# VectorE's order written out in the weight groups and in the layer norm, two more wide groups per FFN, and one sum done by a transfer

## The chip, the cores and the metric

The kernel runs on one NeuronCore of a Trainium2 chip. The metric is the device time of one execution in microseconds, as the median of three executions. The engines are PE (TensorE: matmuls and transposes), ACT (ScalarE), DVE (VectorE), POOL (GpSimd) and SP (SyncE, which only issues transfers here). Each engine has its own list of instructions and works it off in the order in which the list stands.

## The reference

One decoder layer on 256 tokens of width 2048, all in float32: a half-step SwiGLU FFN, a token mixer with two attention branches, a second half-step SwiGLU FFN, and a layer norm after each of the three.

```
def _swiglu(x, w_gate, w_up, w_down):
    return (jax.nn.silu(x @ w_gate) * (x @ w_up)) @ w_down      # 2048 -> 2 x 5632 -> 2048
def _layer_norm(x, g, b):   # (x - mean) * rsqrt(var + eps) * g + b
x = LN1(ALPHA * x + 0.5 * swiglu1(x));  x = LN2(ALPHA * x + mixer(x));  x = LN3(ALPHA * x + 0.5 * swiglu2(x))
```

The last line is a summary of the layer's body. The mixer multiplies by one wide input matrix, runs latent attention and differential attention, gates both and multiplies by an output matrix. Nearly all work is matrix products of the 256 tokens with weights that are read once.

## The kernel before

**Precision.** A float32 product is made of three products of reduced-precision fp32r operands. Each weight tile is split into `hi` (a CAST on ACT, line 150) and `lo` (source minus `hi`, a TENSOR_TENSOR on DVE, line 151). For each k tile of 128 rows PE then runs `triple`: hi by hi (L203), hi by lo (L204), lo by hi (L205), each 512 columns wide. L203 needs only the cast; L204 needs DVE's split too.

**Units and the ring.** Weights come in *units*: a raw tile of 128 x 1024 (two k tiles of 512 columns) or, for a "third slice", 128 x 512 (one k tile). The split results go to a ring of six (hi, lo) pairs, so that the cast of a unit waits until PE has finished the unit six before it. `unit`, `advance` and `look` make the program run the loads three units and the splits four units ahead of the products. The framework's scheduler then sorts each engine's instructions by its own estimates of readiness, within what data and buffers force; the order on an engine is what it leaves, not the order of the source.

**Groups.** Gate and up weights lie in 22 blocks of 512 columns (256 of each). The first two blocks go through plain `project` calls, the other twenty through ten calls of `Hybrid.group`, p = 1 to 10, in each of the two FFNs. A group takes two blocks and both halves of the tokens. Over some k tiles it uses Strassen's seven products instead of eight ("sevens"); the rest are plain units. The order of the units is written as a string: `"15pp6p72q4q3q"` for a *wide* group, `"15pp6p7p2q4q3qq"` for one that is not. A digit is a product, `p` and `q` are plain units of the first and second block. Each product has slices: two of 1024 (k tiles 0 to 7) and, in a wide group, a third of 512 (k tiles 8 and 9, tiles `eraw`). So 6a, 6b, 6c below are the slices of product 6, and p1, p2, p3 are the plain units in order. A wide group has 177 matmuls, one that is not wide 180.

**Sums of weights.** Products 5, 6 and 4 need sums of weight blocks. They are made in place, one DVE addition for each slice (L392). Product 7's sum is made by an accumulating transfer that POOL issues (L394). In the mixer's `small` groups all sums are on DVE.

**Leaving a group.** When a bank of PSUM is finished, DVE adds a saved copy (`gus`, L801), ACT applies silu (`sg`, L785), DVE multiplies (`hb`, L789), and two steps of `later` afterwards `put_h` turns the result with a DVE transpose (L668) and stores it to DRAM by four transfers on POOL's queue (L670). ACT also makes a *seed* (L367): it starts one of the group's banks with minus another bank. `snap` (L354, L355) are copies of banks.

**Layer norm.** `LayerNorm.apply` (DVE: L746 and following, a few 128 x 1 operations with one square root on ACT, then four 128 x 512 operations at L764) normalizes one half of the tokens; the transposes at L633 on PE feed the next stage from it. `finish` (L769, L770) applies gain and bias to the residual's copy; it is called 12 to 15 steps later, and nothing on PE waits for it soon.

## Time and profile before

| quantity | value |
|---|---|
| median of three executions | 1984.71 us (1983.56 to 1985.17) |
| the profiled execution | 1982.88 us, span 1981.1 us |
| PE busy | 1961.8 us, 99% of the span |
| weight loads (PEld) busy | 1623.6 us, 82% |
| DVE busy | 1761.0 us, 89% |
| ACT busy | 1269.4 us, 64% |
| POOL busy | 294.6 us, 15% |
| mean granted clock of PE | 0.997 of full |

PE is busy nearly everywhere, so the time is the number of its instructions times their spacing, plus the places where it waits. The second engine by occupancy is DVE; in the groups of the FFNs it has almost no idle time. A busy share over the whole span hides that: the groups have to be read by themselves.

### The profile page before, as it was taken

What the parts mean: (1) busy time and instruction counts of PE and PEld (TensorE: products, weight loads), DVE (VectorE), ACT (ScalarE), POOL (GpSimd) and SP (SyncE); (2) the same over time, 40 slices, a digit from 0 to 9 for tenths busy, and PEclk for the clock granted to TensorE, in tenths of its full rate; (3) what the DMA queues carried; (4) which work ended last, traced back from release to release, by engine and by line L of the source; (5) the groups of instructions that cost most, each with busy time, mean ns of one, the idle gap of its engine ahead of it and who ended that gap; (6) DMA issues with size and microseconds to landing.
All of it is one profiled execution on the core that took longest, in us unless ns stands there. A gap on an engine that the chain in (4) does not pass through costs nothing.

```text
span 1981.1 us, 25579 instructions
## 1 busy us (share of the span) xinstructions
PE 1961.8 (99%) x8796; PEld 1623.6 (82%) x8796; DVE 1761.0 (89%) x2135; ACT 1269.4 (64%) x1639; POOL 294.6 (15%) x515
## 2 busy tenths in 40 slices
PE   9999999999999999999999999999999999999997
PEld 8888888888888897888888888878888888888886
DVE  7999999999898889998977686699999999998886
ACT  6666666677655666666667864566666666766552
POOL 0211112112100011002223130012112211121000
PEclk9999999999999999999999999999999999999999
DMA  8978888869677666677667677578898878687663
GB/s 314 284 241 279 284 238 247 239 212 329 244 235 243 202 243 225 226 254 260 217 198 256 216 236 264 185 256 271 244 290 260 247 239 244 208 325 251 238 215 124
DMA packets 144594, 484.63 MB, mean 245 GB/s; under 512 B 20640, under 2 KB 20688, under 8 KB 144464
## 3 DMA queue, kind: packets, MB, share of 16 engines
q1 hardware_dynamic: 112752, 389.60, 57.1%
q0 software_dynamic: 31712, 93.41, 17.9%
q8 instruction: 69, 1.13, 0.2%
q14 instruction: 61, 0.50, 0.1%
HBM read 454.08 MB, written 28.84 MB: 244 GB/s over the span
## 4 chain that ended last, share of the span: by engine, by line
PE 89%; DVE 6%; issue 3%; DMA 1%; POOL 0%; ACT 0%; SPq 0%; DVEq 0%; POOLq 0%; ACTq 0%
PE mm L204 28%; PE mm L205 28%; PE mm L203 28%; DVE wring L151 3%; DVE sraw L392 1%; PE tr L203 1%; PE tr L204 1%; PE tr L205 1%; DMA raw<-in_gu_dram 1%; PE tr L633 0%; DMA sraw<-in_wgm_dram 0%; PE tr L1134 0%; PE tr L1207 0%; PE tr L1209 0%; DMA hT<-blocks 0%
## 5 line engine op out<-in xcount | busy, mean ns | idle before, releaser
L150 ACT CAST wring<-raw 128x1024 fp32r<-128x1024 f32 (+2 forms) x475 | 491.4, 1038 | 344.9 <-PE mm L205 244.6
L151 DVE TENSOR_TENSOR wring<-raw,wring 128x1024 fp32r<-128x1024 f32 (+2 forms) x475 | 568.7, 1203 | 112.5 <-ACT wring L150 104.9
L150 ACT CAST wring<-sraw 128x1024 fp32r<-128x1024 f32 x436 | 455.4, 1052 | 207.7 <-PE mm L205 73.2
L151 DVE TENSOR_TENSOR wring<-sraw,wring 128x1024 fp32r<-128x1024 f32 x436 | 525.9, 1222 | 25.5 <-ACT wring L150 21.4
L205 PE MATMUL mm<-wring,h 128*128 128x512 f32 (+2 forms) x1260 | 485.0, 385 | 0.0
L203 PE MATMUL mm<-wring,h 128*128 128x512 f32 (+2 forms) x1260 | 484.7, 385 | 0.0
L204 PE MATMUL mm<-wring,h 128*128 128x512 f32 (+2 forms) x1260 | 484.6, 385 | 0.0
L204 PE MATMUL mm<-wring,xs 128*128 128x512 f32 x776 | 303.1, 391 | 2.5 <-DVE wring L151 2.4
L203 PE MATMUL mm<-wring,xs 128*128 128x512 f32 x776 | 302.3, 390 | 0.0
L205 PE MATMUL mm<-wring,xs 128*128 128x512 f32 x776 | 302.1, 389 | 0.0
L205 PEld LDWEIGHTS mm<-wring,h 128*128 128x128 f32 x1260 | 236.7, 188 | 47.4 <-DVE h L151 0.9
L203 PEld LDWEIGHTS mm<-wring,h 128*128 128x128 f32 x1260 | 236.9, 188 | 46.9 <-ACT h L150 0.4
L204 PEld LDWEIGHTS mm<-wring,h 128*128 128x128 f32 x1260 | 236.8, 188 | 46.9 <-DVE wring L151 0.3
L392 DVE TENSOR_TENSOR sraw<-sraw,sraw 128x1024 f32<-128x1024 f32 x168 | 203.3, 1220 | 3.5 <-DMA sraw<-in_wdv_dram 1.2
L204 PEld LDWEIGHTS mm<-wring,xs 128*128 128x128 f32 x776 | 145.6, 188 | 36.5 <-DVE wring L151 6.5
L203 PEld LDWEIGHTS mm<-wring,xs 128*128 128x128 f32 x776 | 145.7, 188 | 30.2
L205 PEld LDWEIGHTS mm<-wring,xs 128*128 128x128 f32 x776 | 145.7, 188 | 30.0
L204 PE MATMUL mm<-wring,x 128*128 128x512 f32 x348 | 135.7, 390 | 0.5 <-DVE wring L151 0.5
L203 PE MATMUL mm<-wring,x 128*128 128x512 f32 x348 | 135.7, 390 | 0.0
L205 PE MATMUL mm<-wring,x 128*128 128x512 f32 x348 | 135.2, 389 | 0.0
L394 POOL DMA_DIRECT2D sraw<-in_gu_dram x40 | 35.5, 887 | 579.0 <-DVE sraw L392 572.5
L670 POOL DMA_DIRECT2D hT<-blocks x176 | 97.2, 578 | 129.1 <-DVE blocks L668 117.6
(301 smaller groups left out, 2219.6 us busy)
## 6 DMA issues: line engine op xcount, KB each, us to landing
raw<-in_gu_dram SPq DMA_DIRECT2D x167, 512.0 KB, 4.9
sraw<-in_gu_dram SPq DMA_DIRECT2D x160, 512.0 KB, 5.1
raw<-in_dn_dram SPq DMA_DIRECT2D x140, 512.0 KB, 4.6
sraw<-in_gu_dram POOLq DMA_DIRECT2D x40, 512.0 KB, 5.5
sraw<-in_dn_dram SPq DMA_DIRECT2D x36, 512.0 KB, 5.4
hraw<-hT POOLq DMA_DIRECT2D x68, 256.0 KB, 5.3
raw<-in_w_out_dram SPq DMA_DIRECT2D x32, 512.0 KB, 4.4
eraw<-in_gu_dram SPq DMA_DIRECT2D x48, 256.0 KB, 5.1
```

The source lines that it names most:

```text
L150: S.copy(hi, src)
L151: return V.tensor_tensor(out=lo, in0=src, in1=hi.bitcast(F32), op=ALU.subtract)
L203: PE.matmul(o, xh, wh, start=first, stop=False, skip_group_check=again)
L204: PE.matmul(o, xh, wl, start=False, stop=False, skip_group_check=again)
L205: PE.matmul(o, xl, wh, start=False, stop=last, skip_group_check=again)
L392: V.tensor_tensor(out=t, in0=t, in1=R[add[1]][s], op=ALU.add)
L394: nc.gpsimd.dma_start(R["12"][s], source("22", s), accum_op=ALU.add)
L670: nc.gpsimd.dma_start(to.rearrange("(g r) (i f) -> i r g f", g=4, i=4)[i], t[32 * i:32 * (i + 1), :].rearrange("r (g f) -> r g f", g=4))
```

## The change

Five things change in the code.

1. `Hybrid` keeps a list `line` of its DVE splits. `behind_split(n)` puts what is issued inside it behind the n-th last split; this is an edge of order alone, with no data behind it. `split_in_line` puts each split behind the previous one, so that DVE makes them in program order. The additions are put behind a split of some slices earlier.
2. `put_h` is put behind the last split and comes four steps after `hb` instead of two. In the mixer's groups the two closing operations of a group stand behind the last split.
3. `finish` of the layer norm stands behind the last `apply` operation of the second half of the tokens.
4. The condition for a wide group goes from `p % 3 != 1` (p = 2, 3, 5, 6, 8, 9) to `1 < p < KF // 4 - 1` (p = 2 to 9): eight of ten groups of an FFN instead of six.
5. The sum for product 4's third slice leaves DVE; an accumulating transfer on POOL's queue makes it, issued after 6c's split.

Three places show what the scheduler makes of it. Line numbers of the changed kernel are up to 17 higher (L392 becomes L403, L367 L377, L668 L682, L764 L779, L769 and L770 L785 and L786, L785 L802, L789 L806).

The first is ACT and DVE early in group p = 6 of the first FFN. On ACT, before, the cast of 5c (from `eraw`) stands behind p2's cast (from `raw_2013`) and ahead of the seed:

```order
L785 ACTIVATE sg_2005<-gus_2003 128x256
L150 CAST wring_102<-raw_1986 128x1024
L785 ACTIVATE sg_2010<-gus_2008 128x256
L150 CAST wring_120<-raw_2013 128x1024
L150 CAST wring_104<-eraw_468 128x512
L367 ACTIVATE mm_2053<-mm_2018 128x512
```

After, on ACT at the same place (p1 is `raw_1997`, p2 `raw_2024`):

```order
L150 CAST wring_104<-raw_1997 128x1024
L150 CAST wring_102<-raw_2024 128x1024
L802 ACTIVATE sg_2021<-gus_2019 128x256
L377 ACTIVATE mm_2052<-mm_2029 128x512
L150 CAST wring_114<-eraw_468 128x512
```

5c's cast now also stands behind a silu and behind the seed, which have moved ahead of it. On DVE, before, from 5c's sum to 6a's split (`raw_1986` and `raw_2013` are p1 and p2, `raw_2065` is p3, the last row is 6a):

```order
L392 TENSOR_TENSOR eraw_468<-eraw_468 128x512
L789 TENSOR_TENSOR hb_1945<-gus_2008,sg_2010 128x256
L668 STREAM_TRANSPOSE blocks_2025<-hb_1900 128x512
L668 STREAM_TRANSPOSE blocks_2031<-hb_1945 128x512
L151 TENSOR_TENSOR wring_105<-eraw_468,wring_104 128x512
L151 TENSOR_TENSOR wring_103<-raw_1986,wring_102 128x1024
L151 TENSOR_TENSOR wring_121<-raw_2013,wring_120 128x1024
L392 TENSOR_TENSOR sraw_460<-sraw_460,sraw_464 128x1024
L392 TENSOR_TENSOR sraw_461<-sraw_461,sraw_465 128x1024
L392 TENSOR_TENSOR eraw_468<-eraw_468,eraw_469 128x512
L151 TENSOR_TENSOR wring_105<-raw_2065,wring_104 128x1024
L151 TENSOR_TENSOR wring_119<-sraw_460,wring_118 128x1024
```

DVE after, at the same place (the last row is 6a):

```order
L403 TENSOR_TENSOR eraw_468<-eraw_468 128x512
L806 TENSOR_TENSOR hb_1956<-gus_2019,sg_2021 128x256
L151 TENSOR_TENSOR wring_115<-eraw_468,wring_114 128x512
L151 TENSOR_TENSOR wring_105<-raw_1997,wring_104 128x1024
L682 STREAM_TRANSPOSE blocks_2054<-hb_1911 128x512
L682 STREAM_TRANSPOSE blocks_2060<-hb_1956 128x512
L151 TENSOR_TENSOR wring_103<-raw_2024,wring_102 128x1024
L403 TENSOR_TENSOR sraw_460<-sraw_460,sraw_464 128x1024
L403 TENSOR_TENSOR sraw_461<-sraw_461,sraw_465 128x1024
L403 TENSOR_TENSOR eraw_468<-eraw_468,eraw_469 128x512
L151 TENSOR_TENSOR wring_121<-sraw_460,wring_120 128x1024
```

The two transposes have moved from ahead of 5c's split to between p1's and p2's; p3's split no longer stands ahead of 6a's.

The second is PE at the beginning of product 6 in the same group. Before (`wring_118` and `wring_119` are 6a's hi and lo):

```order
L205 MATMUL mm_2095<-wring_120,x_228 128x512
L203 MATMUL mm_2095<-wring_120,x_227 128x512
L204 MATMUL mm_2095<-wring_121,x_227 128x512
L205 MATMUL mm_2095<-wring_120,x_228 128x512
L203 MATMUL mm_2018<-wring_118,xs_336 128x512
L204 MATMUL mm_2018<-wring_119,xs_336 128x512
```

After (`wring_120` and `wring_121` are 6a's, `wring_114` p3's hi):

```order
L205 MATMUL mm_2107<-wring_102,x_228 128x512
L203 MATMUL mm_2029<-wring_120,xs_336 128x512
L203 MATMUL mm_2052<-wring_114,x_212 128x512
L203 MATMUL mm_2107<-wring_114,x_227 128x512
L204 MATMUL mm_2029<-wring_121,xs_336 128x512
L205 MATMUL mm_2029<-wring_120,xs_337 128x512
```

Two products of p3 that need only its cast now stand between 6a's first product and the one that needs DVE's split.

The third is DVE in the layer norm after the mixer (z are the rows, L746 the statistics of the second half). Before:

```order
L746 BN_AGGR mv_10359<-bn_9643 128x2
L770 TENSOR_TENSOR z_9664<-z_9664,gb_9913 128x512
L645 TENSOR_SCALAR ve_10361<-mv_10359 128x1
L769 TENSOR_TENSOR z_9735<-z_9735,gb_9863 128x512
L649 TENSOR_SCALAR w_10365<-mv_10359 128x1
L653 RECIPROCAL y_10367<-sd_10363 128x1
L770 TENSOR_TENSOR z_9735<-z_9735,gb_9966 128x512
L656 SCALAR_TENSOR_TENSOR t_10369<-y_10367,w_10365 128x1
L769 TENSOR_TENSOR z_9735<-z_9735,gb_9863 128x512
L662 SCALAR_TENSOR_TENSOR f_10371<-t_10369,y_10367 128x1
L770 TENSOR_TENSOR z_9735<-z_9735,gb_9966 128x512
L764 TENSOR_SCALAR z_9692<-z_9692,mv_10359,f_10371 128x512 x2
```

After:

```order
L761 BN_AGGR mv_10381<-bn_9665 128x2
L659 TENSOR_SCALAR ve_10383<-mv_10381 128x1
L663 TENSOR_SCALAR w_10387<-mv_10381 128x1
L667 RECIPROCAL y_10389<-sd_10385 128x1
L670 SCALAR_TENSOR_TENSOR t_10391<-y_10389,w_10387 128x1
L676 SCALAR_TENSOR_TENSOR f_10393<-t_10391,y_10389 128x1
L779 TENSOR_SCALAR z_9714<-z_9714,mv_10381,f_10393 128x512 x2
L779 TENSOR_SCALAR z_9792<-z_9792,mv_10381,f_10393 128x512 x2
```

The five operations of `finish` of the first half have left the stretch between the statistics and the normalization of the second half.

The diff, in full:

```diff
--- before.py
+++ after.py
@@ -326,11 +326,21 @@
             V.scalar_tensor_tensor(out=lo, in0=a0, scalar=-1.0, in1=hi.bitcast(F32), op0=ALU.mult, op1=ALU.subtract)
             self.at_[1] = [hi, lo]
 
+    line = []
+
+    def behind_split(n):
+        return tc.issue_after(line[-n].ins) if len(line) >= n else nullcontext()
+
+    def split_in_line(*a):
+        with behind_split(1):
+            line.append(split(*a))
+
     class Hybrid:
 
 
         def __init__(self, x, seven, k_tiles, small=False, extra=None):
 
+            line.clear()
             self.x, self.seven, self.k_tiles, self.small, self.extra = x, seven, k_tiles, small, extra
             self.raws = {n: [act_tile([P, 1024], F32, "sraw") for _ in range(2)] for n in ("11", "12", "22")}
             self.raws["21"] = self.raws["12"] if small else [act_tile([P, 1024], F32, "sraw") for _ in range(2)]
@@ -388,12 +398,15 @@
 
                 def prep():
                     t = R[src][s]
-                    if add is not None and (small or p != 7):
-                        V.tensor_tensor(out=t, in0=t, in1=R[add[1]][s], op=ALU.add)
+                    if add is not None and (small or p != 7) and (p, s) != (4, 2):
+                        with behind_split(s + 1):
+                            V.tensor_tensor(out=t, in0=t, in1=R[add[1]][s], op=ALU.add)
                     if not small and p == 6:
                         nc.gpsimd.dma_start(R["12"][s], source("22", s), accum_op=ALU.add)
                     pair = [v[:, :tiles * 512] for v in next_pair()]
-                    split(*pair, t)
+                    split_in_line(*pair, t)
+                    if (p, s) == (6, 2):
+                        nc.gpsimd.dma_start(t, source("21", s), accum_op=ALU.add)
                     st["pair"] = [v.rearrange("p (g n) -> p g n", g=tiles) for v in pair]
 
                 def now():
@@ -421,7 +434,7 @@
 
                 def prep():
                     pair = next_pair()
-                    split(*pair, st["raw"])
+                    split_in_line(*pair, st["raw"])
                     st["pair"] = [v.rearrange("p (g n) -> p g n", g=G) for v in pair]
 
                 def now():
@@ -433,8 +446,9 @@
                             triple(o, self.x.at(0, k, b), self.x.at(1, k, b), wh[:, g, :], wl[:, g, :],
                                    first and g == 0, last and g == 1, n == 1 or seeded)
                     if last:
-                        done(1, 0, banks["Z"], n2, ALU.add)
-                        done(1, 1, banks["X"], q5, ALU.add)
+                        with behind_split(1) if small else nullcontext():
+                            done(1, 0, banks["Z"], n2, ALU.add)
+                            done(1, 1, banks["X"], q5, ALU.add)
                 unit(load, prep, now)
 
             end = self.k_tiles // G - 1
@@ -702,6 +716,7 @@
             self.z = [[None, None] for _ in range(2)]
             self.counted = [0, 0]
             self.gb = [[None, None] for _ in range(2)]
+            self.applied = {}
 
             def rows(h, b):
                 t = self.z[b][h] = act_tile([P, 1024], F32, "z")
@@ -761,13 +776,14 @@
                 return
             r = rstd(mv[:, 1:2], LN_EPS, 1)
             for c in range(4):
-                V.tensor_scalar(out=zs[c], in0=zs[c], scalar1=mv[:, 0:1], scalar2=r,
-                                op0=ALU.subtract, op1=ALU.mult)
+                self.applied[b] = V.tensor_scalar(out=zs[c], in0=zs[c], scalar1=mv[:, 0:1], scalar2=r,
+                                                  op0=ALU.subtract, op1=ALU.mult)
                 rows_to_quad(zs[c], b, self.x, c, *self.cols)
 
             def finish(c):
-                V.tensor_tensor(out=zs[c], in0=zs[c], in1=gs[c], op=ALU.mult)
-                V.tensor_tensor(out=zs[c], in0=zs[c], in1=bs[c], op=ALU.add)
+                with tc.issue_after(self.applied[1].ins):
+                    V.tensor_tensor(out=zs[c], in0=zs[c], in1=gs[c], op=ALU.mult)
+                    V.tensor_tensor(out=zs[c], in0=zs[c], in1=bs[c], op=ALU.add)
                 self.each(b, c, zs[c])
             for c in range(4):
                 later(12 + c, lambda c=c: finish(c))
@@ -777,7 +793,8 @@
         hT = dram.tile([KF // 4, 2, P, 512], F32, name=f"hT{n}")
 
         def put_h(b, q):
-            turn_out(hb[b, q], hT[q, b])
+            with behind_split(1):
+                turn_out(hb[b, q], hT[q, b])
 
         def half(c, b, up, gate):
             q = c // 2
@@ -788,7 +805,7 @@
             o = (c % 2) * 256
             V.tensor_tensor(out=hb[b, q][:, o:o + 256], in0=up, in1=sg, op=ALU.mult)
             if c % 2 == 1:
-                later(2, lambda: put_h(b, q))
+                later(4, lambda: put_h(b, q))
 
         def gu_done(c, b, bank):
             half(c, b, bank[:, 256:512], bank[:, 0:256])
@@ -845,7 +862,7 @@
                 later(16, lambda: split_h(4))
             hy.group(wgu[2 * p], wgu[2 * p + 1],
                      lambda n, b, bank, snap, op, p=p: sum_done(2 * p + n, b, bank, snap, op),
-                     p % 3 != 1, p > 1)
+                     1 < p < KF // 4 - 1, p > 1)
         ln = LayerNorm(0.5, residual, g, bt, each, nxt, cols, ((24, 26, 48, 50), (94, 97, 100, 103)))
         if n == 1:
             later(70, setup)
```

## The prediction

> **What bounds the kernel now.** I read the page's busy shares first, then the busy time by stretches, the waits of PE, and then the timeline of one group instruction by instruction. The shares, and two stretches inside the FFN groups (columns: PE, PEld, DVE, ACT, POOL busy, clock, DMA share, GB/s):
>
> ```profile
> PE 1961.8 (99%) x8796; PEld 1623.6 (82%) x8796; DVE 1761.0 (89%) x2135; ACT 1269.4 (64%) x1639; POOL 294.6 (15%) x515
> 150.00:200.00 50.00, 50.00 (x223) 41.39 (x222) 49.27 (x51) 33.84 (x41) 7.31 (x12) 1.00 0.89 282
> 1650.00:1700.00 50.00, 49.81 (x220) 40.90 (x219) 49.97 (x57) 34.19 (x44) 8.81 (x13) 1.00 0.77 225
> ```
>
> PE is busy all the time at full clock, and in the groups DVE is too: 49.97 of 50 us. So a matmul less is worth its spacing, if DVE still delivers its splits in time; and DVE has nothing to spare. What PE waits for (line waited for: us in total, times, longest us):
>
> ```profile
> PE tr L633 <- DVE z L764: 4.1, 1, 4.1
> PE mm L204 <- DVE wring L151: 3.0, 8, 1.3
> ```
>
> Only these two count: one wait in the layer norm after the mixer, and eight short ones for a split. Nothing else is to be won except instructions. What the change could lose lies in the same second row: the groups stand on the edge, and a split that comes later is time lost.
>
> **One group, row by row.** Group p = 6 of the first FFN, a wide one before and after. PE (start, us, engine, line):
>
> ```profile
> 253.69 0.39 PE L203 MATMUL mm<-wring,xs 128*128 128x512 f32 x1
> 254.82 0.39 PE L205 MATMUL mm<-wring,xs 128*128 128x512 f32 x1
> 256.18 0.39 PE L205 MATMUL mm<-wring,xs 128*128 128x512 f32 x1
> 265.93 0.39 PE L203 MATMUL mm<-wring,xs 128*128 128x512 f32 x1
> 266.51 0.50 PE L204 MATMUL mm<-wring,xs 128*128 128x512 f32 x1 [0.19 <-DVE wring L151]
> ```
>
> The first is the group's first matmul, the second the last of 1a (its sixth), the third the last of 1b (its twelfth). (256.18 - 253.69) / 11 gives the spacing, 0.2265 us. 265.93 is 6a's first product, 54 spacings after 253.69, so nothing was lost to there. Its L204 follows after 0.58 instead of 0.2265: 0.35 us lost (the row's 0.19 counts from the modelled end). ACT and DVE there:
>
> ```profile
> 255.30 1.05 ACT L150 CAST wring<-raw 128x1024 fp32r<-128x1024 f32 x1 [0.64 <-PE mm L205]
> 256.37 0.42 ACT L785 ACTIVATE sg<-gus 128x256 f32<-128x256 f32 x1
> 256.70 1.03 ACT L150 CAST wring<-raw 128x1024 fp32r<-128x1024 f32 x1
> 257.63 0.62 ACT L150 CAST wring<-eraw 128x512 fp32r<-128x512 f32 x1
> 258.16 0.58 ACT L367 ACTIVATE mm<-mm 128x512 f32<-128x512 f32 x1
> ```
>
> ```profile
> 256.83 0.43 DVE L789 TENSOR_TENSOR hb<-gus,sg 128x256 f32<-128x256 f32 x1
> 257.17 1.30 DVE L668 STREAM_TRANSPOSE blocks<-hb 128x512 f32<-128x512 f32 x2
> 258.39 0.65 DVE L151 TENSOR_TENSOR wring<-eraw,wring 128x512 fp32r<-128x512 f32 x1
> 258.96 2.35 DVE L151 TENSOR_TENSOR wring<-raw,wring 128x1024 fp32r<-128x1024 f32 x2
> 261.23 2.35 DVE L392 TENSOR_TENSOR sraw<-sraw,sraw 128x1024 f32<-128x1024 f32 x2
> 263.50 0.69 DVE L392 TENSOR_TENSOR eraw<-eraw,eraw 128x512 f32<-128x512 f32 x1
> 264.10 1.22 DVE L151 TENSOR_TENSOR wring<-raw,wring 128x1024 fp32r<-128x1024 f32 x1
> 265.23 2.36 DVE L151 TENSOR_TENSOR wring<-sraw,wring 128x1024 fp32r<-128x1024 f32 x2
> ```
>
> DVE goes from 5c's split (258.39) over p1, p2, three sums and p3 to 6a's split (265.23) without a gap. p1's cast (255.30) waits for PE to end 1a: 254.82 + 0.23 = 255.05, and 0.25 later it starts. p2's waits for 1b in the same way.
>
> **New stall in the groups.** In the changed order ACT does, behind 1b: p2's cast, silu, seed, and only then 5c's cast; 5c's split is ahead of everything on DVE. 1b ends at 256.18 + 0.23 = 256.41, p2's cast starts 0.25 later, 256.66. To the next on ACT it takes 0.93 (256.70 to 257.63), the silu 0.33 (256.37 to 256.70), the seed about 0.53 (5c's cast, of the same size, 257.63 to 258.16). So 5c's cast starts at 258.45, and with its 0.62 and some 0.03 of handing over, its split at 259.10, where it was 258.39. The transposes that filled this time on DVE now stand behind it. Behind 5c's split come: itself 0.57 (258.39 to 258.96), p1 and p2 1.135 each (half of 258.96 to 261.23), two transposes 1.22 (257.17 to 258.39), two sums 2.27, the third 0.60. Together 6.93: 6a's split starts at 266.03, and its L204 1.28 later (as 265.23 to 266.51), 267.31. That p3's split has gone from ahead of 6a is counted in this, it had cost 1.13.
>
> PE wants that L204 a little later than before, since two products of p3 now stand behind 6a's first: 265.93 + 3 x 0.2265 = 266.61. So 0.70 us are lost, of it 0.24 already at p1 (split at 259.67, L204 at 260.95; wanted at 253.69 + 31 x 0.2265 = 260.71). All this hangs on the group's own first matmuls, so it comes again in each group with this order: p = 4 to 9. In p = 3 the silu stays ahead of p2's cast, and 0.70 - 0.3 = 0.4 are left. In p = 2 5c's cast stays ahead of p1's, and p = 10 is not wide: nothing. Two FFNs: 2 x (0.4 + 6 x 0.70) = **+9.2 us**. From below it is 0, if 5c's split should still start near 258.4; from above see the rivals.
>
> **Old stalls gone.** The loss of 0.35 at 6a stood in the second of each two wide groups (p = 3, 6, 9), six times in two FFNs; the new sum for these groups replaces it: **-2.1 us**.
>
> **Fewer matmuls.** Four more wide groups with 177 in place of 180: 12 x 0.2265 = **-2.7 us**, since PE sets the pace where it does not wait.
> [...]
>
> **The layer norm after the mixer.** PE's last matmul and its next work, and DVE between:
>
> ```profile
> 1292.29 0.39 PE L205 MATMUL mm<-wring,h 128*128 128x512 f32 x1
> 1296.75 2.08 PE L633 MATMUL tr<-ident,z 128*128 128x128 f32 x11 [4.07 <-DVE z L764]
> ```
>
> ```profile
> 1292.59 0.26 DVE L746 BATCH_NORM_AGGREGATE mv<-bn 128x2 f32<-128x24 f32 x1
> 1292.76 0.63 DVE L770 TENSOR_TENSOR z<-z,gb 128x512 f32<-128x512 f32 x1
> 1293.31 0.14 DVE L645 TENSOR_SCALAR ve<-mv 128x1 f32<-128x1 f32 x1
> 1293.96 0.14 DVE L649 TENSOR_SCALAR w<-mv 128x1 f32<-128x1 f32 x1
> 1295.54 0.69 DVE L770 TENSOR_TENSOR z<-z,gb 128x512 f32<-128x512 f32 x1
> 1296.15 1.92 DVE L764 TENSOR_SCALAR z<-z,mv,f 128x512 f32<-128x512 f32 x4
> ```
>
> Five operations of `finish` (0.55 to 0.6 each, the first at 1292.76, the last at 1295.54) sit between statistics and normalization, 3.56 us in all. The small ones take 0.14 to 0.26; six of them and a square root on ACT and back are 1.0 to 1.8, I take 1.35. So **-2.2 us** (-1.8 to -2.6). `finish` moves to behind, 5 x 0.6 = 3 us more for DVE in the first 20 us of the second FFN; PE is covered there by the ring, and DVE saves the 2.2 as well. If that cover should be gone, 0.8 of it comes back.
>
> **The mixer's groups.** One of the eight waits for a split is large:
>
> ```profile
> 787.01 1.22 DVE L151 TENSOR_TENSOR wring<-raw,wring 128x1024 fp32r<-128x1024 f32 x1
> 788.15 1.22 DVE L392 TENSOR_TENSOR sraw<-sraw,sraw 128x1024 f32<-128x1024 f32 x1
> 789.28 1.22 DVE L151 TENSOR_TENSOR wring<-sraw,wring 128x1024 fp32r<-128x1024 f32 x1
> 790.56 0.50 PE L204 MATMUL mm<-wring,xs 128*128 128x512 f32 x1 [1.29 <-DVE wring L151]
> ```
>
> 1.29 + 0.39 - 0.2265 = 1.45 us. A split of a plain unit (787.01) goes ahead of the sum there; program order turns that round: -1.45, or nothing if the sum waits for its transfer. In the first of these groups a closing operation of 0.66 and a transpose of 0.62 now stand ahead of 6a's sums and splits, 0 to +1.2 by what slack there is, I take the middle. Together **-0.85**.
>
> **The transfer for product 4's sum.** POOL's issue and landing, as now for the sums of product 7:
>
> ```profile
> sraw<-in_gu_dram POOLq DMA_DIRECT2D x40, 512.0 KB, 5.5
> L394 POOL DMA_DIRECT2D sraw<-in_gu_dram x40 | 35.5, 887 | 579.0 <-DVE sraw L392 572.5
> ```
>
> 0.9 + 5.5 = 6.4 us (for twice the bytes). It goes out behind 6c's split. 4c's cast waits for PE to end 2a, six units before: 6c, p3, 7 and 2a are 3 + 12 + 15 + 6 = 36 matmuls, 8.2 us, and 1.3 more from 6c's split to its L204. So 9.5 us cover it: nothing. On POOL's queue the eight stores of `hb` stand ahead, but they follow transposes 7 us earlier. If the cover went, up to 1 us per group would come.
>
> **The sum.** 9.2 - 2.1 - 2.7 - 2.2 - 0.85 = +1.35 us. The profiled execution had 1982.88 (span 1981.1), so it would be 1984.2; the median of the runs is 1.83 above it, 1984.71, and so 1986. A change of less than 0.2%, 4.0 us, can hardly be told from none.
>
> **Rivals.** *PE runs through.* If the new stall does not come, -2.1 - 2.7 - 2.2 - 0.85 = -7.85: 1977. It decides at 5c's split: 0.70 earlier than I have it, about 258.4, where it is now. For it: p3's split is gone from ahead of 6a, one sum is gone, and if DVE lags behind ACT's casts anyway, they don't matter. Against: DVE was free to begin at 257.17 on the transposes, the order now makes it wait for ACT. With half the stall it is -3.3, about the edge. 0.24 for faster.
>
> *DVE's fixed order adds idle time.* Three rows of DVE at the end of a wide group (p = 2):
>
> ```profile
> 117.85 1.23 DVE L151 TENSOR_TENSOR wring<-raw,wring 128x1024 fp32r<-128x1024 f32 x1 [0.19 <-ACT wring L150]
> 121.20 1.22 DVE L151 TENSOR_TENSOR wring<-sraw,wring 128x1024 fp32r<-128x1024 f32 x1 [0.66 <-ACT wring L150]
> 123.51 0.69 DVE L801 TENSOR_TENSOR gus<-mm,snap 128x512 f32<-128x512 f32 x1 [0.48 <-PE mm L205]
> ```
>
> That is 1.33 us idle while DVE waits for casts and banks. A full group has 177 x 0.2265 = 40.1 us, and DVE some 39.5 of work in it (40.1 full as in the second stretch above, less a sum of 0.60). With 0.70 lost it has 40.8 - 39.5 = 1.3 us to be idle. If these waits of 1.33 stay as they are and the wait for 5c of 0.7 comes on top, the group takes 39.5 + 2.0 = 41.5, that is 1.4 lost instead of 0.70: 14 groups by 0.7 are 9.8 more, +11, **1996**. It decides where DVE's idle time per group passes 1.3 us. For it: a fixed order can't fill a wait with something else. Against: much of the idle time was there because DVE was ahead of PE. With half of it +6, 1991. 0.36 for slower.
>
> **Chances and range.** No measurable change 0.40, with 1986 the likeliest and its own range 1982 to 1990; faster 0.24, slower 0.36. From "PE runs through" to "idle time adds up" is 1977 to 1996; a tenth left out at each end: 1979 to 1995.
>
> **What will show it.** In the changed kernel's timeline 6a's L204 should carry a wait for DVE's split in every group p = 3 to 9, of 0.3 to 0.7 us, and DVE a gap of about 0.7 or more ahead of 5c's split, released by ACT. The wait at L633 should fall from 4.1 to about 1.9, the one of 1.3 in the mixer should go. I am wrong if 6a's L204 follows without a gap (1977), or if the wait row of L204 passes 15 us.

## The result

The changed kernel took 1991.45 us (median of six runs, 1989.75 to 1993.14), the kernel before 1984.61 us in the same comparison: a ratio of 1.0038, with a 95% interval of 1.0027 to 1.0049. It is 6.8 us slower. The profiled execution of the changed kernel took 1989.75 us with a span of 1988.0, 6.9 us more than that of before.

The page's busy shares, then two groups of the first FFN by stretches (columns: PE, PEld, DVE, ACT, POOL busy, clock, DMA share, GB/s), then the waits of PE, all of the changed kernel:

```profile
PE 1966.3 (99%) x8784; PEld 1617.9 (81%) x8784; DVE 1763.8 (89%) x2151; ACT 1268.1 (64%) x1659; POOL 311.6 (16%) x535
```

```profile
226.35:267.29 40.94, 40.77 (x179) 33.07 (x177) 39.54 (x45) 28.05 (x38) 10.13 (x16) 1.00 0.90 281
267.29:308.19 40.90, 40.72 (x178) 33.06 (x177) 39.54 (x45) 27.45 (x36) 7.87 (x12) 1.00 0.85 258
```

```profile
PE mm L204 <- DVE wring L151: 3.1, 7, 0.7
PE tr L647 <- DVE z L779: 2.2, 1, 2.2
PE tr L1151 <- ACT dkT L704: 1.3, 1, 1.3
```

The shares tell nothing: 99 and 89% as before. The stretches are from one group's 6a to the next one's: 40.9 us for 177 matmuls, which take 40.1 at a spacing of 0.2265, so 0.8 us is lost in each group. The waits hide that too. They count from a matmul's modelled end, 0.39 us after its start, and a stall of 0.25 us shows as no wait at all. So I added up, for every 512-column matmul, the time from its start to PE's next start beyond 0.2265 us, where it is more than 0.01, by stretches of the span (from 1720 us on there is nothing):

| PE's time beyond the spacing, us | before | after |
|---|---|---|
| start of the kernel (0 to 90) | 1.5 | 1.4 |
| groups of FFN 1 (90 to 410) | 1.4 | 4.8 |
| rest of FFN 1 (410 to 640) | 0.3 | 0.0 |
| first norm and mixer's input products (640 to 985) | 3.6 | 8.4 |
| rest of the mixer (985 to 1270) | 4.6 | 4.4 |
| norm after the mixer (1270 to 1330) | 5.5 | 3.8 |
| groups of FFN 2 (1330 to 1720) | 1.7 | 4.9 |
| all | 18.5 | 27.6 |

That is 9.1 us more, less 2.7 for twelve matmuls fewer: 6.4 of the 6.9 us. Each column is one execution. Stretches that no edit concerns differ by about 1 us between the profiled executions of this document (the start of the kernel has 0.9 to 2.2 us, the rest of the mixer 4.4 to 5.5), so smaller differences in one row mean little.

Group p = 6 of the first FFN in the changed kernel. PE, ACT and DVE (start, us, engine, line):

```profile
254.17 0.39 PE L203 MATMUL mm<-wring,xs 128*128 128x512 f32 x1
260.98 0.40 PE L203 MATMUL mm<-wring,x 128*128 128x512 f32 x1
261.44 0.50 PE L204 MATMUL mm<-wring,x 128*128 128x512 f32 x1
...
266.83 0.39 PE L203 MATMUL mm<-wring,xs 128*128 128x512 f32 x1
267.06 0.61 PE L203 MATMUL mm<-wring,x 128*128 128x512 f32 x2
267.77 0.50 PE L204 MATMUL mm<-wring,xs 128*128 128x512 f32 x1
```

```profile
256.13 2.06 ACT L150 CAST wring<-raw 128x1024 fp32r<-128x1024 f32 x2
258.10 0.41 ACT L802 ACTIVATE sg<-gus 128x256 f32<-128x256 f32 x1
258.41 0.57 ACT L377 ACTIVATE mm<-mm 128x512 f32<-128x512 f32 x1
258.93 0.60 ACT L150 CAST wring<-eraw 128x512 fp32r<-128x512 f32 x1
```

```profile
258.18 0.69 DVE L403 TENSOR_TENSOR eraw<-eraw 128x512 f32<-128x512 f32 x1
258.79 0.42 DVE L806 TENSOR_TENSOR hb<-gus,sg 128x256 f32<-128x256 f32 x1
259.56 0.69 DVE L151 TENSOR_TENSOR wring<-eraw,wring 128x512 fp32r<-128x512 f32 x1 [0.35 <-ACT wring L150]
...
266.50 2.35 DVE L151 TENSOR_TENSOR wring<-sraw,wring 128x1024 fp32r<-128x1024 f32 x2
```

This is the forecast chain. Counted from the group's first matmul (254.17), 5c's split starts at 5.39 us, 6a's at 12.33 and 6a's L204 at 13.60. The prediction had 5.41, 12.34 and 13.62. PE loses 0.24 at p1's L204 (261.44) and 0.26 at 6a's (267.77), 0.11 more at the matmul behind each of the two, and a little in spacings slightly above 0.2265 between; this comes again in every group from p = 4 to 9.

One thing stands elsewhere than the prediction took it to be. 5c's sum starts 4.01 us after the group's first matmul (258.18), where it was 2.50 before (256.19 after 253.69). So DVE was busy until 0.35 us ahead of 5c's split, and with this order on DVE an earlier cast could have brought that split forward by 0.35 us at most.

The norm after the mixer on DVE, and the start of the mixer's input products on DVE and PE:

```profile
1299.55 0.26 DVE L761 BATCH_NORM_AGGREGATE mv<-bn 128x2 f32<-128x24 f32 x1
1300.91 1.91 DVE L779 TENSOR_SCALAR z<-z,mv,f 128x512 f32<-128x512 f32 x4
```

```profile
755.12 1.22 DVE L151 TENSOR_TENSOR wring<-sraw,wring 128x1024 fp32r<-128x1024 f32 x1 [0.88 <-ACT wring L150]
756.27 1.22 DVE L151 TENSOR_TENSOR wring<-raw,wring 128x1024 fp32r<-128x1024 f32 x1
757.40 2.35 DVE L403 TENSOR_TENSOR sraw<-sraw,sraw 128x1024 f32<-128x1024 f32 x2
760.39 2.36 DVE L151 TENSOR_TENSOR wring<-sraw,wring 128x1024 fp32r<-128x1024 f32 x2 [0.63 <-ACT wring L150]
```

```profile
756.40 0.50 PE L204 MATMUL mm<-wring,xs 128*128 128x512 f32 x1 [0.45 <-DVE wring L151]
761.67 0.50 PE L204 MATMUL mm<-wring,xs 128*128 128x512 f32 x1 [0.53 <-DVE wring L151]
```

In the norm 1.36 us lie between statistics and normalization, where 3.56 were. In the mixer DVE now makes two sums and then has nothing it may do (0.63) until the first sum is cast, and PE waits for the split. The starts of successive matmuls give eight losses above 0.3 us in this stretch: 0.31, 0.62 and 0.70 at 754 to 761 us, 0.46 and 0.37 at 797 and 803, 0.62 at 834, 0.83 at 917 and 1.50 at 956. The last is no wait for a split: it is the wait of a transpose (L1151) for ACT, third row of the waits above.

### The profile page after: what moved, and what is told of

The parts are those of the page before. It is cut to its first block, busy times and chain, and to the rows that moved or that the text cites. A ratio compares the mean times of both kernels' runs of the same rounds, so it can differ in the third digit from the quotient of the medians.

```text
span 1988.0 us, 25676 instructions
## 1 busy us (share of the span) xinstructions
PE 1966.3 (99%) x8784; PEld 1617.9 (81%) x8784; DVE 1763.8 (89%) x2151; ACT 1268.1 (64%) x1659; POOL 311.6 (16%) x535
## 3 DMA queue, kind: packets, MB, share of 16 engines
q8 instruction: 68, 1.11, 0.2%
## 4 chain that ended last, share of the span: by engine, by line
PE 83%; DVE 9%; ACT 3%; issue 2%; DMA 2%; POOL 0%; SPq 0%; DVEq 0%; ACTq 0%; POOLq 0%
PE mm L204 27%; PE mm L205 26%; PE mm L203 26%; DVE wring L151 4%; DVE sraw L403 3%; ACT wring L150 2%; DVE blocks L682 1%; PE tr L203 1%; PE tr L205 1%; PE tr L204 1%; DMA sraw<-in_wdk_dram 1%; DMA raw<-in_gu_dram 1%; PE tr L647 0%; DMA turn<-blocks 0%; DVE eraw L403 0%
## 5 line engine op out<-in xcount | busy, mean ns | idle before, releaser
L150 ACT CAST wring<-raw 128x1024 fp32r<-128x1024 f32 (+2 forms) x467 | 481.7, 1037 | 311.2 <-PE mm L205 233.2
L151 DVE TENSOR_TENSOR wring<-raw,wring 128x1024 fp32r<-128x1024 f32 (+2 forms) x467 | 557.9, 1202 | 101.2 <-ACT wring L150 98.9
L204 PE MATMUL mm<-wring,h 128*128 128x512 f32 (+2 forms) x1248 | 480.4, 385 | 1.6 <-DVE wring L151 1.1
L205 PE MATMUL mm<-wring,h 128*128 128x512 f32 (+2 forms) x1248 | 479.9, 385 | 0.0
L203 PE MATMUL mm<-wring,h 128*128 128x512 f32 (+2 forms) x1248 | 479.1, 385 | 0.0
L204 PE MATMUL mm<-wring,xs 128*128 128x512 f32 x776 | 304.4, 392 | 3.2 <-DVE wring L151 1.5
L204 PEld LDWEIGHTS mm<-wring,h 128*128 128x128 f32 x1248 | 234.7, 188 | 51.1 <-DVE wring L151 5.2
L403 DVE TENSOR_TENSOR sraw<-sraw,sraw 128x1024 f32<-128x1024 f32 x168 | 199.3, 1221 | 0.0
L204 PEld LDWEIGHTS mm<-wring,xs 128*128 128x128 f32 x776 | 145.6, 188 | 41.3 <-DVE wring L151 12.0
L204 PE MATMUL mm<-wring,x 128*128 128x512 f32 x336 | 131.8, 392 | 0.9 <-DVE wring L151 0.5
L205 PE MATMUL mm<-wring,x 128*128 128x512 f32 x336 | 130.8, 390 | 0.0
L203 PE MATMUL mm<-wring,x 128*128 128x512 f32 x336 | 129.7, 390 | 0.0
```

What stands on the lines that cost most here:

```text
L150: S.copy(hi, src)
L151: return V.tensor_tensor(out=lo, in0=src, in1=hi.bitcast(F32), op=ALU.subtract)
L203: PE.matmul(o, xh, wh, start=first, stop=False, skip_group_check=again)
L204: PE.matmul(o, xh, wl, start=False, stop=False, skip_group_check=again)
L205: PE.matmul(o, xl, wh, start=False, stop=last, skip_group_check=again)
L403: V.tensor_tensor(out=t, in0=t, in1=R[add[1]][s], op=ALU.add)
```

## Experiments

All ratios are to the kernel before in the same comparison, with 95% intervals; the changed kernel has 1.0038. "Lost" is PE's time beyond the spacing as in the table above.

### The mixer's order taken out

```diff
-    def behind_split(n):
-        return tc.issue_after(line[-n].ins) if len(line) >= n else nullcontext()
+    def behind_split(n, free=False):
+        return tc.issue_after(line[-n].ins) if len(line) >= n and not free else nullcontext()
...
```

The sums and the splits call this with `free=small`, and the two closing operations of a group stand outside it.

> The changed kernel, but with no order edges in the mixer's small groups (splits, sums and closing operations there go where the scheduler puts them, as before); the FFN groups and the layer norm stay as changed. Theory: of the changed kernel's loss, some 4.8 us are waits of PE in the mixer (650 to 1000 us into the span: 8.6 us lost after, 3.7 before) that come from the fixed order in the small groups; so this should be about 4.8 us faster than the changed kernel, 1986 to 1987, and the waits at 755, 761, 797, 803, 833, 916 and 956 us should be gone, while the 1.45 us at 789 us come back. Rival: the mixer's loss comes from something else that was moved (the layer norm's finish, the queue of POOL); then it stays at 1991.

Measured: 1988.01 us, 1.0025 (1.0014 to 1.0036). The mixer's input products lost 4.8 us in place of 8.4 (before: 3.6), the waits at 761, 797 and 803, 834 and 917 us were gone, and 1.2 us at 793 were back. PE's waits of this kernel in the two rows that concern the stretch (the first one has 1.1 us of it at 793):

```profile
PE mm L204 <- DVE wring L151: 1.9, 4, 1.1
PE tr L1151 <- ACT dkT L704: 0.7, 1, 0.7
```

So the fixed order in the mixer's groups is the cause of most of its loss: without it 3.6 us of the 4.8 were gone in that stretch. Not all that was expected went: 0.41, 0.16 and 0.25 us stayed at 755 to 758 us, and 0.88 of the 1.50 at the transpose that waits for ACT. Where these come from was not tried. The whole gained less (about 2.5 us by the ratios); in its profile the kernel's start and the rest of the mixer lost 1.9 us more, with a loss of 0.9 us at 10 us, where PE waited for a cast, among it.

### Only the mixer's closing operations freed

```diff
-                        with behind_split(1) if small else nullcontext():
+                        with nullcontext():
```

> The changed kernel, but the two closing operations of a small group are not put behind the last split. Theory: the closing operations do most of the harm at the mixer's 833 and 916 us, where they stand ahead of the splits of the next group (0.6 and 0.8 us), and not at 755 and 761 us, where sums and casts do; so 1 to 2 us of the mixer's 4.8 come back, 1989.5 to 1990.5. Rival: the closing operations are the whole cause; then 1986 to 1987 as without any order in the mixer.

Measured: 1989.9 us, 1.0030 (1.0019 to 1.0040). The mixer's input products lost 9.0 us. The loss at 834 us went, as expected, but the one at 917 grew to 1.21 and four of 0.23 to 0.38 came at 871 to 886. So freeing the closing operations alone takes nothing away, neither a part as I had it nor all. What is left is the order of splits and sums, by itself or together with the closing operations; that was not separated.

### Casts in program order

```diff
     def split(hi, lo, src, inline=False):
-        S.copy(hi, src)
+        with tc.issue_after(castline[-1].ins) if inline and castline else nullcontext():
+            cast = S.copy(hi, src)
+        if inline:
+            castline[:] = [cast]
...
```

> The changed kernel, and in the groups each ACT cast is put behind the cast before it in the program, so that 5c's cast goes ahead of p1's and p2's. Theory: the 0.51 us lost in each of 12 groups (0.24 at p1, 0.28 at 6a) and 0.28 in two come from 5c's cast standing behind p2's, which waits for PE; 5c's split then starts 1 us earlier, the stalls go, and 6 to 7 us come back in the FFNs (1984.5 to 1985.5, if the mixer loses as much as in the changed kernel). Rival: DVE as a whole is full in the groups and its idle time in a fixed order adds up; then the stall only changes its place and the time stays within 2 us of 1991.

> Both: casts in program order in the FFN groups, no order edges in the mixer's groups. Theory: the two losses lie in different stretches and add up: 1991.5 - 4.8 - 6.5 = about 1980, 4 to 5 us faster than the kernel before. Rival (DVE full in the groups): 1986 to 1987.

Measured, with the mixer's order kept: 1997.94 us, 1.0069 (1.0057 to 1.0082), and with the mixer freed 1989.82 us, 1.0032 (1.0022 to 1.0042). Both theories' numbers were missed: the groups got worse, 6.6 and 7.0 us lost in the two FFNs, with one stall of 0.77 at each 6a. The same group, on ACT and DVE, of the kernel with casts in order:

```profile
259.27 0.58 ACT L383 ACTIVATE mm<-mm 128x512 f32<-128x512 f32 x1 [1.11 <-PE mm L210]
259.77 0.61 ACT L153 CAST wring<-eraw 128x512 fp32r<-128x512 f32 x1
260.27 2.00 ACT L153 CAST wring<-raw 128x1024 fp32r<-128x1024 f32 x2
```

```profile
259.03 0.68 DVE L409 TENSOR_TENSOR eraw<-eraw 128x512 f32<-128x512 f32 x1
260.41 0.69 DVE L156 TENSOR_TENSOR wring<-eraw,wring 128x512 fp32r<-128x512 f32 x1 [0.70 <-ACT wring L153]
261.36 1.23 DVE L156 TENSOR_TENSOR wring<-raw,wring 128x1024 fp32r<-128x1024 f32 x1 [0.26 <-ACT wring L153]
```

5c's cast now stands ahead of p1's and p2's, but still behind the seed, and the seed waits for PE (1.11 us). The seed holds the casts of 5c, p1 and p2, and DVE is idle for 0.70 + 0.26 in place of 0.35. Also, 5c's sum ends on DVE only at 259.71 (259.03 + 0.68), and its cast starts right behind that, at 259.77: even the first place on ACT would not have helped much. What has to come earlier is the sum.

### 5c's sum one split earlier, and the transposes later

```diff
@@ prep() of product 5, slice 1, ahead of its split; the sum is taken out of slice 2
+                    if (p, s) == (5, 1) and wide:
+                        with behind_split(1):
+                            e = V.tensor_tensor(out=R[src][2], in0=R[src][2], in1=R[add[1]][2], op=ALU.add)
+                            line.append(e)
```

As the sum is entered in `line`, 5b's split is put behind it.

> The changed kernel, with 5c's sum one split earlier on DVE (ahead of 5b's split); 5c's cast then stands ahead of p2's cast and the seed on ACT, and DVE does not wait for it. Theory: the gap of 0.35 us on DVE ahead of 5c's split goes in 12 groups and the stalls at p1 and 6a become smaller by as much: about 4 us of the 6.8 come back, 2 to 3.5 us over before. Rival (DVE full): 6 to 7 us over before.

```diff
-                later(4, lambda: put_h(b, q))
+                later(9, lambda: put_h(b, q))
```

> The changed kernel, with put_h nine steps after hb instead of four: the two transposes (1.22 us of DVE) then stand behind p3's split and no longer between 5c's split and 6a's. Theory: in each wide group the chain on DVE from 5c's split to 6a's decides when 6a's L204 can go, so the 0.28 us at 6a goes in 14 groups (3.9 us), and the 0.24 at p1 stays, since 5c's cast comes no earlier: 6.8 - 3.9 = about 3 us over the kernel before. Rival (DVE has as much work per group as PE, and any order loses the same): the stall comes up somewhere else in the group and the time stays 6 to 7 us over before.

> Both edits. Theory: no stall is left in the wide groups; the 0.51 us in 12 groups and 0.28 in two are gone, 6.7 us, and the rest is the mixer's loss of 4.8 against the gains of the norm (2.2) and of 12 matmuls (2.7): within 1.5 us of the kernel before. Rival (DVE full): the group's time stays at 40.6 us or more instead of 40.1, and the whole 4 us or more over before.

Measured, in this order: 1980.28 us, 0.9985 (0.9976 to 0.9994); 1992.47 us, 1.0047 (1.0035 to 1.0060); both together 1981.88 us, 0.9991 (0.9983 to 1.0000). The first edit alone makes the kernel faster than before, by far more than I expected of it: the groups of FFN 1 lost 0.0 us, those of FFN 2 0.2. The second alone loses more than the changed kernel (5.5 and 6.2 us in the groups): the stall at 6a goes, the one at p1 grows to 0.33, and in p = 6 of FFN 1 and two groups of FFN 2 others of 0.5 to 0.6 come. Ahead of those in FFN 1 a cast on ACT had waited 3.28 us for a transfer of weights (249.31; 1.53 at the same place in the changed kernel), so not all of this run's loss need be DVE's order. That the stall comes up elsewhere is what the rival expected of it; the time is 8.6 us over before where the rival had 6 to 7. Both together came out some 2 us faster than before by the medians, a little better than expected. The same place with the sum earlier, PE's first matmul of the group, ACT and DVE:

```profile
252.25 0.39 PE L203 MATMUL mm<-wring,xs 128*128 128x512 f32 x1
```

```profile
255.14 0.60 ACT L150 CAST wring<-eraw 128x512 fp32r<-128x512 f32 x1
255.65 1.05 ACT L150 CAST wring<-raw 128x1024 fp32r<-128x1024 f32 x1
256.61 0.57 ACT L377 ACTIVATE mm<-mm 128x512 f32<-128x512 f32 x1
```

```profile
254.15 0.68 DVE L406 TENSOR_TENSOR eraw<-eraw 128x512 f32<-128x512 f32 x1
254.75 1.22 DVE L151 TENSOR_TENSOR wring<-sraw,wring 128x1024 fp32r<-128x1024 f32 x1
255.88 0.42 DVE L810 TENSOR_TENSOR hb<-gus,sg 128x256 f32<-128x256 f32 x1
256.22 0.68 DVE L151 TENSOR_TENSOR wring<-eraw,wring 128x512 fp32r<-128x512 f32 x1
```

The cast is done under 5b's split, ahead of p2's cast and the seed. Counted from the group's first matmul (252.25), 5c's sum starts at 1.90 us, where it was 4.01 in the changed kernel, and 5c's split at 3.97 without a gap, where it was 5.39. So the split is 1.4 us earlier, more than the 0.24 and 0.26 us by which p1's and 6a's L204 had been late, and all 0.8 us of the group are gone. DVE's own waits in the groups of FFN 1 (95 to 410 us) of the two kernels (us in total, times, longest us), first the changed one, then the one with the sum earlier:

```profile
DVE wring L151 <- ACT wring L150: 11.3, 17, 1.5
```

```profile
DVE wring L151 <- ACT wring L150: 5.9, 16, 1.5
```

DVE has 39.55 us of work for PE's 40.1 in a group, so it may be idle for some 0.55 us. In the changed kernel it waits 0.35 to 0.58 for 5c's cast and, in the groups that I looked at, 0.78 to 0.98 more later in the group, at a split whose cast waits. That is 1.3 us in all in a group of 40.9. With the sum earlier the wait for 5c's cast is gone, two waits of 0.27 and 0.33 later in the group are left, and PE runs through. The sum of the waits had to fall by as much as the group: the work is the same and the group is 0.8 us shorter. What costs PE time is the wait for 5c's cast, which stands where PE soon needs the splits behind it; the waits later in the group leave no stall on PE.

### The norm alone

```diff
+                with tc.issue_after(self.applied[1].ins):
                     V.tensor_tensor(out=zs[c], in0=zs[c], in1=gs[c], op=ALU.mult)
...
```

> The kernel before, with finish of the layer norm behind the second half's apply and nothing else. Theory: the wait of PE at the norm after the mixer falls from 4.1 to about 2.2 us as in the changed kernel, and nothing else moves: 2 us faster than before. Rival: the finish operations that are now later cost the second FFN's start as much as they gave: within 0.5 us of before.

Measured: 1981.17 us, 0.9987 (0.9978 to 0.9995), 2.7 us faster by the medians. The wait at the norm fell from 4.1 to 2.4. The expectation holds.

### Wide groups without the order, the order without more wide groups

```diff
@@ kernel before
-                     p % 3 != 1, p > 1)
+                     1 < p < KF // 4 - 1, p > 1)
@@ and, the other way, in the changed kernel
-                     1 < p < KF // 4 - 1, p > 1)
+                     p % 3 != 1, p > 1)
```

> The kernel before with eight wide groups of ten, and nothing else: no fixed order, all sums of products 5, 6 and 4 on DVE. Theory: DVE has 40.15 us of work for 40.1 of PE in each of eight groups in succession, so every group behind the second is late as p = 3, 6, 9 were, by 0.35 us or more: 14 x 0.35 to 0.9 less the 2.1 of before and 2.7 for 12 matmuls, 0 to +8 us, I take +4 (1.002). Rival (only the fixed order does harm): -2.7 + 8 x 0.35, the time of before.

> The changed kernel with the old condition, six wide groups of ten. Theory: after each group that is not wide DVE has 3 us to spare and catches up, so the stalls do not come in each group but in the second of a pair at most, 0.3 to 0.5 us, as before; the FFNs are then as before, the mixer loses its 4.8 and the norm gives 2.2: +2 to +3 us (1.0010 to 1.0015). Rival (the stall is only 5c's cast behind PE, whatever DVE has to do): 0.5 us in each of 12 wide groups, +5 to +6 us (1.003).

Measured: 1985.58 us, 1.0009 (1.0001 to 1.0018), and 1985.77 us, 1.0010 (1.0002 to 1.0019). Wide groups alone lose 3.3 + 3.6 us in the groups (before 1.4 + 1.7), more than the 2.7 they save: +1.1. The loss is 0.35 us at 6a and 0.11 behind it, now in each wide group from p = 3 on, and it does not grow from group to group; so the +4 that I took was too much, and "the time of before" a little too little. With the order and only six wide groups the groups lose 1.4 + 1.4 as before, so the stall is not tied to the order alone: where DVE can catch up in a group that is not wide, it is no larger than it was (in FFN 1 of the kernel before DVE was idle for 1.56 of 40.80 us in p = 7, which is not wide, and for 0.53 of 40.61 in p = 6). That is what the theory expected, and the time, 1.4 us over before by the medians, is a little under its +2 to +3. The 8.3 us of the mixer's stretch remain there.

### The transfer taken back

The edit is against the kernel with 5c's sum earlier.

```diff
-                    if add is not None and (small or p != 7) and (p, s) not in ((4, 2), (5, 2)):
+                    if add is not None and (small or p != 7) and (p, s) != (5, 2):
@@
-                    if (p, s) == (6, 2):
-                        nc.gpsimd.dma_start(t, source("21", s), accum_op=ALU.add)
```

> 5c's sum one split earlier, but product 4's third sum on DVE again instead of by a transfer. Theory: a wide group then has 39.55 + 0.60 = 40.15 us of work for DVE and 40.1 for PE; with successive wide groups nothing is left for DVE to be idle, and 0.1 to 0.5 us per group are lost in 14 groups: 1.5 to 7 us slower than with the transfer, 0.999 to 1.002 of the kernel before. Rival (only the wait for 5c's cast matters, DVE's amount of work does not): as with the transfer, 0.9985.

Measured: 1981.73 us, 0.9986 (0.9976 to 0.9995), the same as with the transfer (1980.28 us, 0.9985). The rival was right. The groups lost 0.3 and 0.5 us, with DVE busy all the time. 200 us of FFN 1's groups, in this run and in the one with wide groups alone:

```profile
180.00:380.00 200.00, 200.00 (x883) 165.44 (x882) 199.26 (x225) 136.46 (x176) 37.59 (x60) 1.00 0.86 263
180.00:380.00 200.00, 199.03 (x873) 163.23 (x872) 197.71 (x222) 137.89 (x176) 35.34 (x57) 1.00 0.86 262
```

Both kernels have the same wide groups and the same sums on DVE, in a different order: 40.15 us of DVE's work in a group. With the order left to the scheduler DVE waits 0.42 us in a group for a bank that PE has not finished, and the groups lose 3.3 and 3.6 us; with this fixed order it does not wait in these 200 us, and the groups lose 0.3 and 0.5. So it was the order, not the amount of DVE's work, that cost time. The reserve is used up, though: a stall of 0.18 us stands at 6a of the last wide group of each FFN (387.22 and 1670.99 us), and an order with any wait in it would show at once. The adding transfer is worth nothing measurable once the waits are gone.

### The better version

The sum of 5c earlier, and no fixed order in the mixer's groups.

> 5c's sum one split earlier, as in the run with that alone (0.9985 of the kernel before, no wait left in the FFN groups), and no order edges in the mixer's groups (some 3.6 us less of PE's waits there in the run with that alone). Theory: the two lie in different stretches and add up: 3 to 3.6 us less than with 5c alone, 0.9967 to 0.9970 of the kernel before, about 1977. Rival: without the fixed order in the mixer something else there becomes late, and it stays at 0.998 to 0.9985.

Measured: 1977.02 us, 0.9968 (0.9955 to 0.9980). It is faster than both kernels, 7.3 us less than the one before by the medians. The two edits add up as expected: the groups lost 0.0 and 0.6 us, the mixer's input products 4.4. The groups of FFN 1, and the longest waits of PE that are left:

```profile
142.00:402.00 260.00, 260.00 (x1149) 215.29 (x1148) 256.48 (x286) 181.26 (x234) 52.47 (x81) 1.00 0.88 265
```

```profile
PE tr L651 <- DVE z L783: 2.4, 1, 2.4
PE mm L204 <- DVE wring L151: 1.5, 2, 1.1
```

## Why the prediction was right or wrong

The time lay in the range (1979 to 1995), the likeliest case was no measurable change, and one term of the sum failed. The likeliest value, 1986, and its own range (1982 to 1990) missed the measured 1991.45; what held was the wide range that the rivals had given. That the rival at half its size had 1991 is luck: the FFN groups, where it put the loss, lost what the main sum said, and the rest came from the mixer.

- **The new stall in the groups, +9.2, and the old ones gone, -2.1:** right, together +7.1; the groups' stretches lost 9.7 us after and 3.1 before, +6.6. The chain came out to within 0.02 us at each of its three points in p = 6. But the cause as I told it was half of it. 5c's cast does hold the chain, but it could not come much earlier, because 5c's sum had moved back on DVE from 2.50 to 4.01 us, which I had left out; putting the cast earlier made it worse, putting the sum earlier took the loss away. For the same reason DVE's gap ahead of 5c's split was 0.35 us (0.58 in p = 5) and not the 0.7 or more that I named as a sign. The two transposes stand in the chain to 6a as I counted them, but moving them away only shifted the loss. The sign in the wait of 6a's L204 did not show: the view has no wait of PE in these groups, and the stalls of 0.26 to 0.28 us stand in the spacing alone. And the run with six wide groups shows that the chain costs 0.7 us per group only where no group between gives DVE time to catch up.
- **Fewer matmuls, -2.7:** the table of losses and this count give the total to 0.5 us. The run with 0.60 us more on DVE in each wide group was no slower, so DVE's added work was not time here: PE set the pace (busy 200.00 of the 200 us shown above) with weight loads busy 83% of the time (165.44 us) and DVE 99.6% (199.26 us).
- **The norm, -2.2:** right; the wait went from 4.1 to 2.2 us, and the norm alone made the kernel before 2.7 us faster by the medians (1 to 4 us by the interval).
- **The mixer's groups, "Together -0.85":** this is the step that failed. It was +4.8 (3.6 to 8.4), 5.65 us off, nearly the whole difference between +1.35 and +6.8. I costed one wait that I saw before and one group in which something was put ahead. In place of the wait of 1.45 there were two of 0.46 and 0.37, and the first group lost 1.6 us in place of 0 to 1.2; but the same order made new waits of 0.62 and 0.83 in other groups too, which I had not looked at. The run without that order took 3.6 us of the stretch away, the one with freed closing operations none. A loss of 1.50 at a transpose that waits for ACT is in the 4.8 as well; 0.88 of it stayed without the order, and about 0.8 of the first group's 1.6, so for these the cause is open.
- **The transfer, 0:** right, as far as the runs show: taking it back changed nothing in the kernel with 5c's sum earlier.
- **The forecast case.** "No measurable change" had 0.40, slower 0.36; it was slower. The rival "DVE's fixed order adds idle time" named the mechanism of the mixer's loss, but placed it in the FFN groups, at +11. The rival "PE runs through" had named what decides there, the place of 5c's split: with the split 1.4 us earlier PE ran through. Without the stall and without a gain in the mixer the sum is -2.1 - 2.7 - 2.2 = -7.0 us, and the better version came out 7.3 us under before by the medians (1977.02) and 6.4 by the ratio.

## What to carry to other kernels

In this kernel a fixed order on a busy engine was to be judged by where the engine waits, not by its work: for every operation that stands in it, ask whether its input comes from another engine that has just been given the data (sum, cast, split here), and put something else between. DVE ran at 199.3 of 200 us and PE lost nothing in them; with 97% and two waits per group PE lost 2%. Stalls of 0.26 us stood in no list of waits here; the spacing of the starts showed them. When an order is written for one place and the code is shared, cost all places that share it: here the loss came where the order was not meant to help.

## What was not expected of the hardware

After the wait at the norm PE can run at half its clock for some microseconds, so that the wait costs more than its length. In the kernel with both edits in the groups (sum earlier, transposes later) it was so for 6.8 us (1300.20 to 1307.02), with 0.427 us from matmul to matmul. PE's last matmul ahead of the wait and the transposes behind it, and two stretches after (the clock is the third figure from the right):

```profile
1296.06 0.39 PE L205 MATMUL mm<-wring,h 128*128 128x512 f32 x1
1298.87 1.69 PE L651 MATMUL tr<-ident,z 128*128 128x128 f32 x12 [2.43 <-DVE z L783]
```

```profile
1300.00:1303.00 3.00, 2.44 (x10) 1.76 (x9) 3.00 (x6) 3.00 (x10) 0.46 (x1) 0.53 0.16 61
1303.00:1306.60 3.60, 3.60 (x10) 2.83 (x9) 3.60 (x9) 3.60 (x10) 0.64 (x2) 0.50 0.38 146
```

In the changed kernel the granted clock was 0.50 from 1302.48 to 1305.89 us, in the kernel before from 1297.38 to 1300.79, 3.41 us each. Of ten profiled executions of this document six, these three among them, had a granted clock of 0.99 from 980 to 1320 us and four 1.00. Among the four is the kernel without the mixer's order, where PE had waited 3.1 us; the wait of 2.43 above was followed by 6.8 us at half clock. So the length of the wait does not decide by itself, and the time that one execution loses to it differs by up to some 2 us (an estimate: in the kernel above ten steps from matmul to matmul, 1302.58 to 1306.84, took 4.26 us, and 2.27 at the spacing of 0.2265).

The clock fell 0.63 us after PE's first transpose behind the wait in the kernel before (1296.75 to 1297.38), 0.97 in the changed one (1301.51 to 1302.48) and 1.33 in the kernel with both edits (1298.87 to 1300.20). In the last PE had stood still for 2.43 us and then had transposes of 128 columns alone. Whether the pause is enough by itself or these transposes have a part in it, no run here separates.
